# Hybrid pooling and attention block: a gate projection in another PSUM bank ahead of the last attention values, and the residual of the output projection loaded into its result tiles

## The chip, the cores and the metric

The kernel runs on one core of a Trainium2 chip. Its time is the device time of one execution in microseconds (us). The kernel before has a median of 2409.88 us over three runs (2409.58 to 2410.88). An execution that was recorded by the profiler gives the trace that all rows below come from. Engines are named as in the profile: PE is the matrix engine, PEld its weight load, DVE the vector engine, ACT the activation engine, POOL the general engine, SP the engine that issues most of the DMA transfers. SPq is the queue of SP: it issues in order, and a transfer that has to wait for a buffer holds up the transfers behind it.

## What is computed

One decoder block on x of 2048 positions by 1024 channels, all in float32. Cut to what matters here:

```python
h = rmsnorm(x, attn_norm)
z = h @ w_in                       # pool channels | q | k | v | gate_pool | gate_attn
gates = sigmoid(z[..., o4:] + b_gate)
g_pool, g_attn = gates[..., :D_MODEL], gates[..., D_MODEL:]
a = pool_mixer(u_pool, w_pool, pool_scale)      # causal means of 2, 4, 8, 16, minus the input
b = swa_sink_attention(q, k, v, sinks)          # window 128, 16 query heads, 2 key/value heads
x = x + (g_pool * a + g_attn * b) @ w_out
h = rmsnorm(x, ffn_norm)
up = causal_depthwise_conv(h @ w_up, conv_w, conv_b)
gate, val = up[..., :D_FF], up[..., D_FF:]
x = x + (silu(gate) * val) @ w_down
```

## The kernel before

**Chunks and precision.** The sequence goes through in two chunks of 1024 positions (`c` = 0 and 1). Activations lie with channels on the 128 partitions. To hold float32 precision every operand of a large product is split into a high part (a cast on ACT) and a low part (a subtraction on DVE), and each product is three matmuls, high by high, high by low, low by high (`mm3`, lines 257 to 263; `product`, lines 1166 to 1173). So every weight slab costs ACT and DVE work before PE can use it: `split` (lines 245 and 246), `halved` (358 and 359), the steps `second` and `fourth` of `Blocks` (374 to 379 and 386 to 388), `parted` (1043 and 1044) for activations.

**Attention.** `mixer` (from line 1656) runs 32 items, four groups of eight blocks (the last group is `group == 3`, its blocks are `n` = 0 to 7). For an item, `scores` makes the matmuls (873 to 879) and on DVE the mask, the maximum and two small operations (882 to 889; the last of these, line 889, is what `scores` returns as `chain`), then the exponentials on ACT (892) and the normalisation on DVE (898). `probabilities` of the item before transposes on PE (906), splits on ACT and DVE (908, 911) and makes a masked copy on POOL (914). `values` of the item two back multiplies with the values (934) into a bank of tag `"a"` and ACT copies it out (941). Between them stand fillers: projections such as `gated` (1007), which multiplies 24 matmuls into a bank of tag `"f"` (`project`, 689 to 697), and DVE and ACT then make tanh and `combine` from it (1015, 1016, 1023, 1024).

**Gates with fewer products.** The gates of the remaining channel tiles are computed two at a time by seven half-size products instead of eight (`Gates`, a subclass of `Up`: `one` to `seven`, lines 1191 to 1222). Each unit holds one bank of tag `"f"` from `one` to `seven`. Their right sides are differences of input blocks: `right_t1` (1133 to 1138) and `right_t2` to `right_t4`. In the first chunk two units start inside the last attention group, so both `"f"` banks are held when `gates` (from line 1411) begins. That function's head holds, in this order: the last filler (the plain gate `pg` of channel tile 4, first half; first chunk only), the last `probabilities`, the second half of `right_t1`, the last `values`, the loads of two input tiles, then the products `four`, `early`, `three` and so on. `values` of the item before the last stands ahead of all that, in `mixer` (1752).

**Order of the work.** The text's order gives priorities. A scheduler places each instruction of each engine in a fixed order when its inputs and its buffer are free by the scheduler's own reckoning, so an instruction whose buffer comes free late is placed behind others that stand after it in the text. `tc.issue_after(ins)` puts what is traced inside it behind `ins` on that instruction's engine.

**Output projection.** `out_proj` (1055 to 1116) runs two halves of 512 positions (`n`) by eight channel tiles (`m`). For each it loads a 128 by 512 residual `xr` of 256 KB from `xT` (1064, 1065, pool `fp`, tag `"F"`, four buffers), takes the split weights of `w_out` (three raw buffers of tag `"R"`, loaded three slabs ahead), makes 24 matmuls (1086), adds the residual on DVE (1090), scales into the result tile `xg` on ACT (1091; four tiles of 128 by 2 by 1024, pool `up_`, tag `"U"`, 19 buffers), squares it (647, 650), and stores it to `x2d` (1098). In the first chunk's first half it also makes the weights of two later units and stores them (1067 to 1076), which adds loads of `w_up` and stores to `kept`.

Of the kernel before, what the change touches and what calls it, by code (L numbers as in the profile page):

```python
# [16 lines left out]
F32 = mybir.dt.float32  # L17
# [9 lines left out]
P = 128  # L27
D = 1024
S = 2048
T = 1024  # L30
# [188 lines left out]
def block_kernel(ctx: ExitStack, tc: tile.TileContext, x, xT, pos, vec, qkn, w_poolT, w_pool, w_q, w_kv,  # L219
# [787 lines left out]
    def gated(c, ct, n, hs, ta, st):  # L1007
        if ("d", ct) not in st:
            st["pg"] = stream.get("pg", ct, later=later)
            st["t"] = fp.tile([P, T], F32, "F")  # L1010
            st["d", ct] = fp.tile([P, T], F32, "F")
            load(st["d", ct], dd[ct])
        pg, c_ = project(hs, st["pg"], n)
        d, t = st["d", ct][:, c_], st["t"][:, c_]
        V.tensor_mul(pg, pg, rB[:, c_])
        A.activation(t, pg, AF.Tanh, scale=0.5, bias=hbg[:, ct:ct + 1])
        later.append(lambda: combine(ct, n, t, ta, st))
# [37 lines left out]
    def out_proj(c, ms, mixes):  # L1055

        xg = [up_.tile([P, 2, T], F32, "U") for _ in range(4)]
        norms = []
        heads = [Kept(f) for f in PRE]
        for n in range(2):  # L1060
            acc = fp.tile([P, 512], F32, "F")
            c_ = slice(n * 512, (n + 1) * 512)
            for m in range(KT):
                xr = fp.tile([P, 512], F32, "F")
                load(xr, xT[m * P:(m + 1) * P, c * T + n * 512:c * T + (n + 1) * 512])
                w = stream.get("out", m)
                for f, at in PRE.items() if c == n == 0 else ():
                    if m == at:
                        raw = up_.tile([P, 2, 8, P], F32, "U")
                        load(raw[:, 0], w_up[f])  # L1070
                        load(raw[:, 1], w_up[FT + f])
                        made = Blocks([raw[:, 0], raw[:, 1]])
                    elif at < m < at + 3:
                        made.step(2)
                    elif m == at + 3:
                        made.store(f)
                if n == 0 and m == 3:
                    mixes[0] = mixed(0)
                if n == 0 and m > 3:
                    ms[7 - m].append(parted(mixes.pop(7 - m)[:, :, N1]))  # L1080
                if n == 1 and m >= 6:
                    heads[m - 6].fetch("A11", "A12")
                if n == 1 and m == 7:
                    stream.ahead().step(1)
                po = ps.tile([P, 512], F32, "f")
                mm3(po, [(w[:, 0, k, :], w[:, 1, k, :], ms[k // 2][n][:, 0, k % 2, :],
                          ms[k // 2][n][:, 1, k % 2, :])
                         for k in (6, 7, 4, 5, 2, 3, 0, 1)])
                x2 = mp.tile([P, 512], F32, "M")
                V.scalar_tensor_tensor(x2, po, 0.5, xr, op0=ALU.mult, op1=ALU.add)  # L1090
                A.activation(xg[m // 2][:, m % 2, c_], x2, AF.Identity,
                             scale=vc[:, V_FN + m:V_FN + m + 1])
                if m < 7 or n == 0:
                    square_in(acc, x2, m == 0)
                else:
                    sq = mp.tile([P, 512], F32, "M")
                    A.square(sq, x2)
                load(x2d[m][:, c_], x2)
                stream.part(stream.used + 2)
                if n == 1 and m == 1:  # L1100
                    norms[0]()
                if n == 1 and m == 3:
                    pb, b = norms[1](), {}
                if n == 1 and m >= 3 and m < 7:
                    right_first(xg, b, m - 3, pb)

            accs = [acc, sq] if n else [acc]

            def stats(n=n, accs=accs):
                rstd(accs, r2[:, 4 * n:4 * n + 4])  # L1110

            def whole(n=n):
                return spread(r2[:, 4 * n:4 * n + 4], None)

            norms += [stats, whole]
        return xg, b, norms[2:], heads
# [294 lines left out]
    def gates(c, units, b, xg, last_probabilities, last_values, last_filler):  # L1411
# [20 lines left out]
        else:  # L1432
            weights(1, 1)
            last_filler()
        last_probabilities()
        right_t1(xg, b, None, (1,))
        if c > 0:
            u2.two()
        last_values()
        run_later(9)  # L1440
        xg += [load_input(c, j) for j in (2, 3)]
        parts(0, "S3", "S2")
# [213 lines left out]
    def mixer(c, hs, kvw):  # L1656
# [49 lines left out]
        for i in range(len(items)):  # L1706
            group, n = divmod(i, NB)
            chain = scores(items[i])
            if i + 2 < len(items):
                load_queries(items[i + 2])  # L1710
            if i > 1:
                values(items[i - 2])
            run_later(0)
            fills = fillers(c, group)[n]
            last = chain
            for j, f in enumerate(fills):
                if i > 0 and j == (len(fills) > 1):
                    last = probabilities(items[i - 1], chain)
                if j == (len(fills) > 1):
                    run_later(2, last)  # L1720
                filler(*f, c, hs, ta, st)
            if group == 3:
                if c == 0:
                    if n == 0:
                        stream.fetch(stream.used + 2)
                    for f, steps in enumerate(({1: 1, 2: 2, 3: 1}, {5: 1, 6: 1})):
                        if n in steps:
                            units[f].w.step(steps[n])
                            units[f].w.store(units[f].f)
                    if n == 4:  # L1730
                        stream.fetch(stream.used + 1)
                elif n < 5:
                    if n == 2:
                        stream.fetch(stream.used + 2)
                    if n > 2:
                        units[n - 3].w = Kept(units[n - 3].f)
                        units[n - 3].w.fetch("A11", "A12")
                elif n == 5:
                    units[2].w = stream.get("gates", units[2].f)
                    units[2].w.step(1)  # L1740
                else:
                    units[n - 6].w.fetch("S1", "S4")
                if n in (4, 5):
                    xg.append(load_input(c, n - 4))
                if n == 5:
                    run_later(9)
                if n == 6:
                    scale_input(xg[0], 0)
                    right_t1(xg, b, None, (0,))
                if n == 7:  # L1750
                    scale_input(xg[1], 1)
        values(items[-2])
        run_later(9)
        return gates(c, units, b, xg, lambda: probabilities(items[-1]), lambda: values(items[-1]),
                     lambda: filler("pg", 4, 0, c, hs, ta, st))

    high, low = split_weights.last
    with tc.issue_after(low):
# [102 lines left out]
```

## Time and profile before

| | us |
|---|---|
| median of three runs | 2409.88 |
| the profiled execution's own time | 2411.6 |
| its span on the core | 2409.9 |
| PE busy in it | 2375.1 (99%) |
| DVE busy | 1885.8 (78%) |
| ACT busy | 1180.4 (49%) |
| POOL busy | 177.0 (7%) |

The span holds, in order: the first chunk's mixer to about 500 us, its output projection to 596, its up projection to about 1021 and the down projection to about 1233, and then the same for the second chunk, whose output projection lies between 1682 and 1771 us. In the rows of the profile, `[1.71 <-ACT U L245]` behind an instruction means that its engine was idle for 1.71 us before it and that an ACT instruction of line 245 ended that. "L" numbers are lines of the kernel. PEclk is the clock that PE was granted, 1.00 being full. An idle time under 0.15 us isn't shown as such.

### The profile page before, as it was taken

What the parts mean: (1) busy time and instruction counts of PE and PEld (TensorE: products, weight loads), DVE (VectorE), ACT (ScalarE), POOL (GpSimd) and SP (SyncE); (2) the same over time, 40 slices, a digit from 0 to 9 for tenths busy, and PEclk for the clock granted to TensorE, in tenths of its full rate; (3) what the DMA queues carried; (4) which work ended last, traced back from release to release, by engine and by line L of the source; (5) the groups of instructions that cost most, each with busy time, mean ns of one, the idle gap of its engine ahead of it and who ended that gap; (6) DMA issues with size and microseconds to landing.
All of it is one profiled execution on the core that took longest, in us unless ns stands there. A gap on an engine that the chain in (4) does not pass through costs nothing.

```text
span 2409.9 us, 30324 instructions
## 1 busy us (share of the span) xinstructions
PE 2375.1 (99%) x11120; PEld 1970.3 (82%) x11120; DVE 1885.8 (78%) x2916; ACT 1180.4 (49%) x2169; POOL 177.0 (7%) x122
## 2 busy tenths in 40 slices
PE   9999999999999999999999999999999999999999
PEld 8888887877888888788888888878888888888887
DVE  8687887876977777799945867787588777779994
ACT  7455455454555555543522544554546445554431
POOL 1123111000000000000002142200000000000000
PEclk9999999999999999999999999999999999999999
DMA  9767778588222333545244576665742222228421
GB/s 342 245 202 236 228 218 274 192 288 295 103 79 79 93 117 114 178 173 183 88 155 141 171 220 195 200 201 198 230 167 93 95 80 79 79 71 288 140 70 53
DMA packets 162597, 400.77 MB, mean 166 GB/s; under 512 B 14224, under 2 KB 50576, under 8 KB 152720
## 3 DMA queue, kind: packets, MB, share of 16 engines
q1 hardware_dynamic: 157664, 390.26, 47.8%
q0 software_dynamic: 4352, 8.39, 2.2%
q8 instruction: 87, 1.43, 0.2%
q14 instruction: 62, 0.51, 0.1%
q10 hardware_dynamic: 432, 0.19, 0.0%
HBM read 264.17 MB, written 134.61 MB: 165 GB/s over the span
## 4 chain that ended last, share of the span: by engine, by line
PE 53%; DMA 2%; DVE 2%; ACT 1%; issue 0%; POOL 0%; DVEq 0%; ACTq 0%; POOLq 0%; SPq 0%
PE f L262 11%; PE f L1170 11%; PE t L1170 6%; PE f L1637 4%; PE a L1637 4%; PE s L1637 4%; PE t L1637 4%; PE a L1170 3%; PE a L934 1%; PE a L262 1%; PE s L873 1%; DMA tad<-U 1%; PE t L906 0%; DMA U<-xT 0%; DMA F<-dd 0%; DMA U<-xd 0%
## 5 line engine op out<-in xcount | busy, mean ns | idle before, releaser
L262 PE MATMUL f<-U,U 128*128 128x512 f32 (+1 forms) x2880 | 674.5, 390 | 9.4 <-ACT U L245 5.3
L262 PEld LDWEIGHTS f<-U,U 128*128 128x128 f32 x2880 | 529.1, 188 | 120.5 <-ACT U L245 6.6
L1170 PE MATMUL f<-U,U 128*128 128x512 f32 x1872 | 446.9, 390 | 4.1 <-ACT Q L1188 3.8
L1170 PEld LDWEIGHTS f<-U,U 128*128 128x128 f32 x1872 | 350.4, 188 | 80.1 <-ACT Q L1188 6.0
L1236 DVE SCALAR_TENSOR_TENSOR M<-F,vc,M 128x1024 f32<-128x1024 f32 x176 | 225.1, 1281 | 140.8 <-ACT M L1233 140.5
L1170 PE MATMUL t<-U,U 128*128 128x512 f32 x1332 | 316.7, 391 | 0.6 <-ACT Q L1188 0.6
L1170 PEld LDWEIGHTS t<-U,U 128*128 128x128 f32 x1332 | 250.9, 189 | 53.3 <-ACT Q L1188 1.2
L358 ACT CAST U<-R 128x1024 fp32r<-128x1024 f32 x147 | 153.8, 1053 | 86.5 <-DVE R L387 42.3
L1170 PE MATMUL a<-U,U 128*128 128x512 f32 x756 | 183.9, 390 | 0.0
L359 DVE TENSOR_TENSOR U<-R,U 128x1024 fp32r<-128x1024 f32 x147 | 179.2, 1220 | 3.0 <-ACT U L358 3.0
L1170 PEld LDWEIGHTS a<-U,U 128*128 128x128 f32 x756 | 141.3, 188 | 29.4 <-ACT Q L1188 0.2
L1170 PE MATMUL f<-U,M 128*128 128x512 f32 x624 | 151.3, 390 | 2.1 <-DVE F L1214 2.0
L892 ACT ACTIVATE Q<-s,st,rq 128x128 f32<-128x128 f32 x256 | 113.7, 455 | 63.6 <-DVE st L889 63.2
L1170 PEld LDWEIGHTS f<-U,M 128*128 128x128 f32 x624 | 116.8, 188 | 27.7 <-DVE F L1214 3.6
L914 POOL TENSOR_SCALAR_AFFINE_SELECT M<-M 128x1024 fp32r<-128x1024 f32 x64 | 94.7, 1479 | 381.2 <-DVE st L894 245.0
L1222 ACT COPY F<-f 128x512 f32<-128x512 f32 x52 | 30.5, 586 | 182.7 <-PE f L1170 182.7
L1595 ACT CAST U<-U 128x1024 fp32r<-128x1024 f32 x76 | 79.0, 1051 | 83.4 <-PE s L1637 21.5
L1233 ACT ACTIVATE M<-F,vc 128x1024 f32<-128x1024 f32 x88 | 109.4, 1243 | 2.0 <-DVE F L1218 0.5
L1596 DVE TENSOR_TENSOR U<-U,U 128x1024 fp32r<-128x1024 f32 x76 | 91.9, 1218 | 2.8 <-ACT U L1595 2.6
L1595 ACT CAST F<-U 128x1024 fp32r<-128x1024 f32 x44 | 46.2, 1050 | 93.0 <-PE a L1637 63.5
L941 ACT COPY U<-a 128x512 f32<-128x512 f32 x64 | 37.6, 587 | 109.4 <-PE a L934 109.1
L1188 ACT COPY Q<-f 128x512 f32<-128x512 f32 x104 | 60.8, 585 | 50.8 <-PE f L1170 50.8
(281 smaller groups left out, 3728.5 us busy)
## 6 DMA issues: line engine op xcount, KB each, us to landing
R<-w_up SPq DMA_DIRECT2D x80, 512.0 KB, 3.7
actd<-M SPq DMA_DIRECT2D x44, 512.0 KB, 2.6
U<-w_down SPq DMA_DIRECT2D x88, 256.0 KB, 4.7
U<-actd SPq DMA_DIRECT2D x88, 256.0 KB, 5.0
qd<-U SPq DMA_DIRECT2D x64, 256.0 KB, 3.7
Q<-qd SPq DMA_DIRECT2D x64, 256.0 KB, 4.9
R<-w_out SPq DMA_DIRECT2D x32, 512.0 KB, 5.1
U<-kept_S SPq DMA_DIRECT2D x12, 1024.0 KB, 6.3
```

The source lines that it names most:

```text
L262: nc.tensor.matmul(out, a, b, start=(i == 0), stop=(i == n - 1))
L358: A.copy(t[:, 0], raw)
L359: V.tensor_sub(t[:, 1], raw, t[:, 0].bitcast(F32))
L892: A.activation(pr[:, h, :], sc[:, h, 0:P], AF.Exp, bias=nm[:, h:h + 1], scale=it["rq"][:, h:h + 1], accum_out=rs[:, h:h + 1])
L914: G.affine_select(own.rearrange("p a h q -> p (a h) q"), pa.bitcast(F32).rearrange("p a h q -> p (a h) q"), pattern=[[0, 8], [1, P]], base ...
L1170: nc.tensor.matmul(bank, a[:, x, k, :], b[k // 2][:, y, k % 2, :], start=(first and i == 0), stop=(i == 11), skip_group_check=True)
L1188: Up.last = A.copy(t, bank).ins
L1233: A.activation(y, u[:, 2:], AF.Identity, bias=cw[:, 3, m:m + 1], scale=cw[:, 2, m:m + 1])
L1236: V.scalar_tensor_tensor(y, u[:, j:j + T], cw[:, j, m:m + 1], y, op0=ALU.mult, op1=ALU.add)
L1595: A.copy(hi, src)
L1596: V.tensor_sub(lo, src, hi.bitcast(F32))
L1637: nc.tensor.matmul(into[m], u[:, 0, c_], v[:, 1], start=(first and j == 0), stop=(k == n - 1 and j == 2), skip_group_check=True)
```

## The change

Three edits, with the lines that they touch:

1. The last filler of the first chunk, the plain gate, projects into a bank of tag `"a"` in place of `"f"`. The `values` of the item before the last move from ahead of it to behind the last `probabilities`, in both chunks.
2. In the last attention group, the weight steps of the first two units are traced under `issue_after(chain)`; the second step of unit 1 moves from `n` = 6 to `n` = 7; the first half of `right_t1` moves from `n` = 6 to `n` = 7, behind `chain`. The move of `right_t1` holds for both chunks, the steps for the first.
3. In `out_proj`, both chunks, the 16 residual loads of 256 KB into `"F"` tiles go. In their place four loads of 1 MB fill the result tiles `xg` themselves, the first at the function's start and the others at `m` = 0, 2 and 4 of the first half; the addition reads the residual from there, and the scaling writes over it in place.

```diff
-        pg, c_ = project(hs, st["pg"], n)
+        pg, c_ = project(hs, st["pg"], n, st.pop("tag", "f"))
...
+        def residual(j):
+            load(xg[j], xT[2 * j * P:(2 * j + 2) * P, c * T:(c + 1) * T]
+                 .rearrange("(k p) t -> p k t", p=P))
+
+        residual(0)
         heads = [Kept(f) for f in PRE]
         for n in range(2):
...
             for m in range(KT):
-                xr = fp.tile([P, 512], F32, "F")
-                load(xr, xT[m * P:(m + 1) * P, c * T + n * 512:c * T + (n + 1) * 512])
+                if n == 0 and m % 2 == 0 and m < 6:
+                    residual(m // 2 + 1)
                 w = stream.get("out", m)
...
-                V.scalar_tensor_tensor(x2, po, 0.5, xr, op0=ALU.mult, op1=ALU.add)
+                V.scalar_tensor_tensor(x2, po, 0.5, xg[m // 2][:, m % 2, c_], op0=ALU.mult,
+                                       op1=ALU.add)
...
         last_probabilities()
+        last_values(-2)
+        run_later(9)
         right_t1(xg, b, None, (1,))
         if c > 0:
             u2.two()
-        last_values()
+        last_values(-1)
...
-                    for f, steps in enumerate(({1: 1, 2: 2, 3: 1}, {5: 1, 6: 1})):
+                    for f, steps in enumerate(({1: 1, 2: 2, 3: 1}, {5: 1, 7: 1})):
                         if n in steps:
-                            units[f].w.step(steps[n])
+                            with tc.issue_after(chain):
+                                units[f].w.step(steps[n])
...
                 if n == 6:
                     scale_input(xg[0], 0)
-                    right_t1(xg, b, None, (0,))
                 if n == 7:
+                    with tc.issue_after(chain):
+                        right_t1(xg, b, None, (0,))
                     scale_input(xg[1], 1)
-        values(items[-2])
-        run_later(9)
-        return gates(c, units, b, xg, lambda: probabilities(items[-1]), lambda: values(items[-1]),
-                     lambda: filler("pg", 4, 0, c, hs, ta, st))
+        return gates(c, units, b, xg, lambda: probabilities(items[-1]),
+                     lambda i: values(items[i]),
+                     lambda: filler("pg", 4, 0, c, hs, ta, dict(st, tag="a")))
```

## The prediction

> **What bounds the kernel.** I read the page first, then PE's waits in the stretch that the change touches, then the timelines of PE, DVE, POOL and SP around each wait, and last the granted clock.
>
> ```profile
> span 2409.9 us, 30324 instructions
> ...
> PE 2375.1 (99%) x11120; PEld 1970.3 (82%) x11120; DVE 1885.8 (78%) x2916; ACT 1180.4 (49%) x2169; POOL 177.0 (7%) x122
> ```
>
> PE is the bound: 2409.9 - 2375.1 leaves 34.8 us in the whole span in which it did nothing. So an edit can gain only by removing PE's idle time or time at a reduced clock, and loses by making either. The profiled execution took 2411.6 us, 1.7 more than its span and 1.7 more than the median of 2409.9; I make the sum as differences and apply it to the median. PE's waits between 340 and 600 us, from the last attention group of the first chunk to the end of its output projection (total, times, longest):
>
> ```profile
> PE f L262 <- ACT U L245: 5.3, 3, 1.9
> PE a L934 <- POOL M L914: 2.8, 1, 2.8
> PE f L1170 <- ACT Q L1188: 2.5, 2, 2.0
> PE f L262 <- DVE U L246: 2.1, 5, 0.9
> PE a L934 <- DVE M L911: 0.6, 1, 0.6
> PE f L1170 <- DVE U L1044: 0.3, 1, 0.3
> ```
>
> These are 13.6 of the 34.8 us, in a ninth of the span. Three places make them: the gates' head, the products behind it (L1188, L1044), and the output projection (L245, L246).
>
> **Part 1: the gates' head.** PE's timeline:
>
> ```profile
> 396.74 0.50 PE L934 MATMUL a<-M,U 128*128 128x512 f32 x1 [0.58 <-DVE M L911]
> 400.03 1.22 PE L934 MATMUL a<-M,U 128*128 128x512 f32 x2 [2.79 <-POOL M L914]
> ...
> 436.43 5.60 PE L262 MATMUL f<-U,U 128*128 128x512 f32 x24
> ```
>
> The two waits stand inside `values` of the item before the last. The 24 matmuls at 436.43 are the last filler, the plain gate. The text puts it ahead of those values, but both `"f"` banks belong to units 0 and 1 until a unit's `seven`, so it was placed 40 us late. While PE waits for POOL it has 5.6 us of work that only lacks a bank. Why the values were late:
>
> ```profile
> 392.32 0.69 DVE L882 COPY_PREDICATED s<-causal,s 128x512 f32<-128x512 uint8 x1
> ...
> 394.79 1.22 DVE L1137 TENSOR_TENSOR U<-U 128x1024 f32<-128x1024 f32 x1
> 395.93 0.15 DVE L889 TENSOR_TENSOR st<-st,vc 128x4 f32<-128x4 f32 x1
> 396.00 0.68 DVE L911 TENSOR_TENSOR M<-t,M 128x512 fp32r<-128x512 f32 x1
> ```
> ```profile
> 396.81 3.16 POOL L914 TENSOR_SCALAR_AFFINE_SELECT M<-M 128x1024 fp32r<-128x1024 f32 x1 [8.71 <-DVE st L894]
> ```
>
> From the mask (L882) to L889 DVE needed 3.6 us, because `right_t1` and weight steps were threaded in between; L911 came behind that, and POOL's select behind L911. The waits also cost clock. The next table cuts time into stretches of 3.41 us that end where the granted clock changes (PE busy, PEld, DVE, ACT, POOL, then PEclk):
>
> ```profile
> 395.78:399.20 3.42, 0.88 (x3) 0.19 (x1) 3.42 (x7) 3.27 (x12) 2.39 (x1) 1.00 0.57 170
> 399.20:402.60 3.40, 2.57 (x8) 1.97 (x9) 2.26 (x4) 1.16 (x3) 0.78 (x1) 0.50 1.01 395
> 402.60:406.03 3.43, 3.43 (x9) 2.66 (x9) 1.71 (x2) 2.32 (x3) 1.09 (x1) 0.50 0.53 203
> ...
> 419.68:423.09 3.41, 1.83 (x8) 1.52 (x9) 3.38 (x5) 3.41 (x4) 0.00 (x0) 1.00 0.01 1
> 545.97:549.38 3.41, 1.46 (x5) 0.93 (x6) 3.41 (x6) 3.41 (x7) 0.00 (x0) 1.00 1.06 435
> 549.38:552.80 3.42, 3.42 (x10) 2.65 (x9) 2.76 (x4) 1.29 (x3) 0.00 (x0) 0.50 0.99 401
> ```
>
> A stretch in which PE was busy 0.88 or 1.46 us of 3.4 is followed by half clock; one with 1.83 us isn't. At half clock PE was busy for 2.57 + 3.43 = 6.0 us here, of which half, 3.0 us, is lost. The head thus loses 0.58 + 2.79 + 3.0 = 6.4 us.
>
> With the gate in an `"a"` bank its matmuls start where PE began to wait, at 396.2, and last 5.6 us, past the end of the second wait at 400.0. DVE reaches L889 earlier as well, by up to the 1.22 us of L1137 and the weight steps behind it. So all 6.4 us go. What is late next: the gate no longer stands at 436, nor as a cushion, and PE comes earlier to the products behind the head, which waited 2.5 + 0.3 us there, with DVE all but full:
>
> ```profile
> 416.00:430.00 14.00, 11.21 (x47) 8.33 (x46) 13.28 (x14) 9.55 (x11) 0.00 (x0) 1.00 0.51 143
> ```
> ```profile
> 405.61 0.38 SPq L239 DMA_DIRECT2D U<-xT  x1
> ```
>
> PE loses 6.4 us less and does 5.6 us more there, so it is 0.8 us earlier at those products, with the gate behind it. The load at 405.61 that feeds their right sides waits for a `"U"` tile that the last values release, and so moves with PE; but DVE has to make the right sides in 94% of its time. The gate's own DVE work, three operations of the shape of L911 (0.68 us each), moves there too. I put 1.0 us of new wait on it. Bounds: nothing new and the old 2.8 us gone as well (a gain of 9.2), or DVE holds PE up for nearly all of it (a gain of 1). The value taken, 6.4 - 1.0 = **5.4 us gained**, is nearest to the row of the waits as they are, since their causes move with PE.
>
> The small moves. The `values` moved behind the transposes are four matmuls and one ACT copy; the bank that they need is that of unit 1's `two`, which DVE (L1200) reads while the gate runs. The last values need the gate's bank, which is free after the gate's tanh; PE has the moved values to do meanwhile. Unit 1's second step takes its 0.5 MB store with it; behind that on SPq stand a `w_ga` load for a later unit and an input load that waits on a buffer anyhow. `right_t1` issues no DMA; its tile is needed by `four`, which stands behind the gate and the values. All of these at nothing, hidden by the gate's 5.6 us; without that cover the delay of `right_t1`, two operations like L1137, would show as about 2.4 us.
>
> **Part 2: the output projection of the first chunk.** From SPq, the landing view of those two transfers (`xT`, then `w_out`), DVE, and PE:
>
> ```profile
> 521.96 0.94 SPq L239 DMA_DIRECT2D F<-xT  x1
> 522.94 0.58 SPq L239 DMA_DIRECT2D R<-w_out  x1
> ```
> ```profile
> DMA to landing us min/median/max: 8.3/8.3/8.3
> ```
> ```profile
> DMA to landing us min/median/max: 8.6/8.6/8.6
> ```
> ```profile
> 530.36 0.69 DVE L1090 SCALAR_TENSOR_TENSOR M<-f,F 128x512 f32<-128x512 f32 x1 [5.60 <-issue]
> ```
> ```profile
> 533.41 0.73 PE L262 MATMUL f<-U,U 128*128 128x512 f32 x2 [1.71 <-ACT U L245]
> 534.31 5.75 PE L262 MATMUL f<-U,U 128*128 128x512 f32 x24 [0.17 <-DVE U L246]
> 540.36 5.28 PE L262 MATMUL f<-U,U 128*128 128x512 f32 x22 [0.29 <-DVE U L246]
> 547.58 0.74 PE L262 MATMUL f<-U,U 128*128 128x512 f32 x2 [1.94 <-ACT U L245]
> 548.66 4.61 PE L262 MATMUL f<-U,U 128*128 128x512 f32 x12 [0.34 <-DVE U L246]
> ```
>
> The residual for `m` = 4 was issued at 521.96 and landed at 530.3; DVE's addition starts at 530.36 after 5.60 us of idle time that no engine ended. Behind it in DVE's and ACT's order stand the scaling and the splits of the next weights, so PE waits at 531.7. DVE then works off the backlog and PE waits again at 545.6, which is followed by 3.42 us at half clock, 1.7 us lost. Sum: 1.71 + 0.17 + 0.29 + 1.94 + 0.34 + 1.7 = 6.2 us. With `xg[2]` loaded from `m` = 2 on, its addition no longer waits, DVE has no backlog, and the second wait and the clock loss go. The first wait doesn't go wholly: `w_out` for `m` = 6 landed at 522.94 + 8.6 = 531.5, and its split can't start before; a first cast and subtraction, each taken as L911's 0.68, put it at 532.9, so 1.2 us stays. **Gain 5.0 us.** The bytes are the same, 4 MB per chunk, but 2 MB of the second half's loads now stand in the first, where there is little room:
>
> ```profile
> 511.00:534.00 23.00, 21.29 (x94) 17.12 (x92) 14.89 (x22) 11.72 (x19) 0.00 (x0) 1.00 1.00 373
> ```
>
> ```profile
> 491.33 1.25 SPq L239 DMA_DIRECT2D U<-w_up  x2
> ```
>
> The DMA engines are full from 511 to 534 at 373 GB/s; 1 MB more ahead of `w_out` costs 2.8 us there. The first load stands ahead of the `w_up` loads issued at 491.33, 20 us before that stretch, the second right behind them, and the third takes the place of the 256 KB loads of `m` = 1 to 3, so I expect the fourth at most to stand in the way. Bounds: a gain of 7 (all, with restarts), a loss of 9 (the last rival).
>
> **Part 3: the second chunk and the rest.** Its waits between 1540 and 1610 us:
>
> ```profile
> PE f L1170 <- DVE F L1214: 1.7, 1, 1.7
> PE a L934 <- POOL M L914: 1.0, 1, 1.0
> PE t L906 <- DVE Q L898: 0.7, 1, 0.7
> ```
>
> No plain gate stands here, so only the order changes. L898's wait should go with `right_t1` out of the chain; the others may shift. Gain 0.5, bounds 1.7 lost to 1.7 gained. Its output projection waits nowhere that the loads could relieve. The wait of the first chunk's other L245 (5.3 - 1.71 - 1.94 = 1.7 us) is behind weight steps that already came after their chain: nothing, within 2 us either way.
>
> **Sum.** 5.4 + 5.0 + 0.5 = 10.9 us off 2409.9: **2399.0 us**, by itself good for 2394.5 to 2403. What this kernel's measurement can tell from no change is about 0.2%, 4.8 us, so the border of faster is 2405.1.
>
> **Rivals.**
> *The loads stay in the way.* The fourth 1 MB load delays `w_out` of `m` = 6 by 2.8 us, and what the addition gains the split loses: part 2 gives nothing. For it: DMA share 1.00. Against it: the four loads can be issued before 511 if `"U"` tiles are free. 2409.9 - 5.9 = 2404.0. Chance 0.14.
> *The head gives little.* DVE (13.28 of 14 us) sets the pace behind the head, or the gate is still placed late. Part 1 gives 1: 2403.4. Chance 0.13. Both of these together: 2408.4, chance 0.06.
> *The clock isn't the waits' doing.* Then 3.0 + 1.7 us of half clock stay: 2399.0 + 4.7 = 2403.7. Against it: both stretches follow the two emptiest ones. Chance 0.04. The Trainium skill, TensorE: Matmul & The Clock Gate, section Part 1, lets the clock fall after at least one idle window of about 3.4 us; by that rule waits of 2.79 and 1.94 us would cost none. The trace has the length of the window but not the wholly idle one: PE was busy 0.88 and 1.46 us in them.
> *Slower.* The third or fourth load finds no free `"U"` tile, since mixes, split weights and stored weight blocks hold them, and SPq stands still until stores have landed. Behind it stands `w_out`. It decides from about 3 us of standstill: `w_out` then lands at 531.5 + 3 + 2.1 (0.75 MB more at 373 GB/s) = 536.6, the wait at 531.7 grows from 1.7 to about 6 and brings half clock for two stretches (3.4), and DVE's backlog keeps the second wait and adds 1.2. Part 2 loses 4.3 + 3.4 + 1.2 = 8.9, less parts 1 and 3: 2409.9 + 8.9 - 5.9 = 2412.9. Against it: the last unit's products release the eight tiles of T1 to T4 by the end of the mixer. Chance 0.07.
>
> **Numbers.** Forecast 0.56, rivals 0.14, 0.13, 0.06, 0.04, 0.07. The rivals at 2403.4 to 2404.0 lie near the border, a third of them beyond it: faster 0.78, within 0.2% 0.14, slower 0.08. The range goes from 2394 to 2408.
>
> **What would show it.** Right: the 24 matmuls of the gate stand in an `"a"` bank ahead of the values at about 396 to 402; no half clock between 395 and 410 or 540 and 560; L1090 at `m` = 4 not idle for 5 us; xT loads mostly ahead of 515. Wrong: a `w_out` load issued later than 525 or landing later than 534 for `m` = 6; a wait of over 4 us behind the head; a new half-clock stretch anywhere.

## The result and the profile after

The changed kernel has a median of 2415.66 us over 13 executions (2413.23 to 2418.73), the kernel before, run beside it, 2410.66 us (2408.69 to 2413.36). The ratio is 1.0022, its 95% interval 1.0013 to 1.0030: about 5 us slower, where 11 us faster was forecast and the range ended at 2408. The execution that was profiled took 2413.23 us, the lowest of the 13, with a span of 2411.5; its trace thus shows 1.6 us of the difference, and what the other executions have beyond that it can't show.

The page, first lines:

```profile
span 2411.5 us, 30292 instructions
...
PE 2374.3 (98%) x11120; PEld 1969.9 (82%) x11120; DVE 1886.6 (78%) x2916; ACT 1180.3 (49%) x2169; POOL 176.4 (7%) x122
```

PE is still the bound, with 37.2 us of idle time where it had 34.8. Lines behind the edits have other numbers: the residual's addition is L1096 now (it was L1090), the scaling L1098 (L1091), the product L1177 (L1170), `scale_input` L1415 (L1408). PE's timeline at the gates' head:

```profile
396.14 5.60 PE L262 MATMUL a<-U,U 128*128 128x512 f32 x24
...
406.38 0.74 PE L934 MATMUL a<-M,U 128*128 128x512 f32 x2 [0.21 <-POOL M L914]
...
424.23 0.80 PE L1177 MATMUL f<-U,U 128*128 128x512 f32 x1 [7.51 <-ACT U L1043]
```

The first two rows are as predicted: the plain gate stands at 396 in its new bank, and of the waits of 0.58 and 2.79 us in the values 0.21 is left. The third is new, a wait of 7.51 us behind the head, at a product of the units. It costs clock too. The stretches of 3.41 us (PE busy, PEld, DVE, ACT, POOL, then PEclk):

```profile
417.53:420.94 3.41, 0.00 (x0) 0.00 (x0) 1.04 (x1) 2.19 (x2) 0.00 (x0) 1.00 1.06 327
420.94:424.36 3.42, 0.13 (x1) 0.13 (x1) 3.42 (x4) 3.12 (x3) 0.00 (x0) 0.50 0.91 261
424.36:427.77 3.41, 2.69 (x6) 1.80 (x7) 3.41 (x4) 2.90 (x3) 0.00 (x0) 0.50 0.31 97
427.77:431.18 3.41, 3.41 (x10) 2.49 (x8) 3.41 (x4) 2.37 (x4) 0.00 (x0) 0.50 0.16 65
```

A stretch in which PE did nothing is followed by three at half clock, in the first of which PE was still almost idle. They hold 0.13 + 2.69 + 3.41 = 6.2 us of busy time, half of it lost: 3.1 us, as much as before at its own place (3.0). What PE waited for is seen by going back from it: ACT's and DVE's timelines, then SPq's.

```profile
417.62 2.19 ACT L1415 ACTIVATE U<-U,vc 128x1024 f32<-128x1024 f32 x2 [3.98 <-DMA U<-xT]
421.05 2.19 ACT L1415 ACTIVATE U<-U,vc 128x1024 f32<-128x1024 f32 x2 [1.25 <-DMA U<-xT]
```
```profile
407.33 0.74 DVE L1024 SCALAR_TENSOR_TENSOR U<-F,vc,U 128x512 f32<-128x512 f32 x1
419.90 1.23 DVE L1153 TENSOR_TENSOR M<-U,U 128x1024 f32<-128x1024 f32 x1 [11.83 <-ACT U L1415]
```
```profile
398.80 0.32 SPq L239 DMA_DIRECT2D kept_A<-M  x1
404.20 0.32 SPq L239 DMA_DIRECT2D kept_S<-U  x1
408.09 0.32 SPq L239 DMA_DIRECT2D xd<-U  x1
408.51 0.58 SPq L239 DMA_DIRECT2D tad<-U  x1
409.18 2.59 SPq L239 DMA_DIRECT2D U<-xT  x2
```

DVE, of which the prediction feared that it would be full, was idle for 11.83 us: it had nothing to make right sides from. The loads of the two input tiles were issued at 409.2 and 409.9 and took 8.4 and 11.2 us to land, until 417.6 and 421.1. In the kernel before the first was issued at 395.96, behind one store and one weight load, and the second at 405.61 (shown above), and each landed within 5.5 us:

```profile
390.69 0.33 SPq L239 DMA_DIRECT2D kept_A<-M  x1
391.08 0.42 SPq L239 DMA_DIRECT2D R<-w_ga  x1
395.96 0.38 SPq L239 DMA_DIRECT2D U<-xT  x1
397.92 0.33 SPq L239 DMA_DIRECT2D kept_S<-U  x1
```

The store at the head of both lists, `kept_A<-M`, is that of unit 1's second step. That step was moved behind the chain, its DVE work (L375) now starts at 398.08, and everything behind its store on SPq stands until then. Behind it follow two more stores that wait for DVE. `kept_S<-U`, of 1 MB, is that of unit 1's next step, `weights(1, 1)` at the head of `gates`; it works on what the second step leaves and was pushed back with it, from 397.92 to 404.20. `xd<-U` is the plain gate's, behind L1024 at 407.33, and comes earlier in the queue than before. SPq waited 12.4, 5.0 and 3.5 us for the DVE work of these three. In the kernel before the first input load stood ahead of `kept_S` and the second ahead of `tad`; now both stand behind all four stores.

The output projection of the first chunk. SPq, the landing view of `w_out` for `m` = 6, ACT and DVE:

```profile
525.43 1.39 SPq L239 DMA_DIRECT2D U<-xT  x1
526.87 1.35 SPq L239 DMA_DIRECT2D R<-w_out  x1
```
```profile
DMA to landing us min/median/max: 11.5/11.5/11.5
```
```profile
538.44 1.14 ACT L245 CAST U<-R 128x512 fp32r<-128x512 f32 x2 [4.77 <-DMA R<-w_out]
```
```profile
529.73 0.69 DVE L1096 SCALAR_TENSOR_TENSOR M<-f,U 128x512 f32<-128x512 f32 x1 [2.74 <-PE f L262]
```

The addition at `m` = 4 no longer waits for its residual (its 2.74 us are for PE), but the fourth 1 MB load stands in front of `w_out` for `m` = 6, which lands at 538.4 instead of 531.5, and now ACT waits 4.77 us for that. PE's waits from 490 to 620, the kernel before and the kernel after:

```profile
PE f L262 <- ACT U L245: 3.6, 2, 1.9
PE f L262 <- DVE U L246: 1.7, 4, 0.9
```
```profile
PE f L262 <- ACT U L245: 4.5, 2, 2.6
PE f L262 <- DVE M L1096: 0.8, 1, 0.8
PE f L262 <- DVE U L246: 0.8, 2, 0.4
```

5.3 us became 6.1, and one stretch at half clock (533.58 to 537.00) took the place of another: nothing won. In the second chunk the three waits of 3.4 us between 1540 and 1610 shrank to one:

```profile
PE a L1177 <- ACT Q L1195: 0.7, 1, 0.7
```

So the traces give PE 3.3 us more of waits from 340 to 470 us (11.6 where it had 8.3), 0.8 more in the first output projection, and 3.7 less from 1500 to 1800 (0.7 where it had 4.4). The rest of the 2.4 us of added idle time stands elsewhere, 1.2 of it ahead of 340 us.

### The profile page after: what moved, and what is told of

It is laid out like the page before. It is cut to its first block, busy times and chain, and to the rows that moved or that the text cites. A ratio compares the mean times of both kernels' runs of the same rounds, so it can differ in the third digit from the quotient of the medians.

```text
span 2411.5 us, 30292 instructions
## 1 busy us (share of the span) xinstructions
PE 2374.3 (98%) x11120; PEld 1969.9 (82%) x11120; DVE 1886.6 (78%) x2916; ACT 1180.3 (49%) x2169; POOL 176.4 (7%) x122
## 4 chain that ended last, share of the span: by engine, by line
PE 55%; DVE 1%; DMA 1%; ACT 0%; issue 0%; POOL 0%; SPq 0%; DVEq 0%; ACTq 0%; POOLq 0%
PE f L262 12%; PE f L1177 12%; PE t L1177 7%; PE f L1646 4%; PE a L1646 4%; PE s L1646 4%; PE t L1646 4%; PE a L1177 4%; PE a L934 1%; PE a L262 1%; PE s L873 1%; PE t L906 1%; DMA U<-made_pg 0%; DVE F L990 0%; ACT Q L892 0%; DMA U<-w_down 0%
## 5 line engine op out<-in xcount | busy, mean ns | idle before, releaser
L1177 PE MATMUL f<-U,U 128*128 128x512 f32 x1872 | 449.9, 391 | 9.6 <-ACT U L1043 7.5
L1177 PEld LDWEIGHTS f<-U,U 128*128 128x128 f32 x1872 | 352.6, 189 | 85.8 <-ACT U L1043 7.9
L1177 PE MATMUL t<-U,U 128*128 128x512 f32 x1332 | 315.0, 390 | 0.5 <-ACT Q L1195 0.4
L1177 PEld LDWEIGHTS t<-U,U 128*128 128x128 f32 x1332 | 249.5, 188 | 53.9 <-ACT Q L1195 1.2
L1177 PE MATMUL a<-U,U 128*128 128x512 f32 x756 | 184.3, 390 | 1.4 <-ACT Q L1195 1.4
L1177 PEld LDWEIGHTS a<-U,U 128*128 128x128 f32 x756 | 141.2, 188 | 31.6 <-ACT Q L1195 2.3
L1177 PE MATMUL f<-U,M 128*128 128x512 f32 x624 | 151.0, 389 | 0.3 <-DVE F L1221 0.3
L1177 PEld LDWEIGHTS f<-U,M 128*128 128x128 f32 x624 | 117.0, 188 | 25.0 <-DVE F L1221 0.8
L246 DVE TENSOR_TENSOR U<-R,U 128x512 fp32r<-128x512 f32 x122 | 82.9, 705 | 9.0 <-ACT U L245 8.7
```

Source lines behind the costliest of these rows:

```text
L246: low = V.tensor_sub(lo[:, t], src[:, t], hi[:, t].bitcast(F32))
L1177: nc.tensor.matmul(bank, a[:, x, k, :], b[k // 2][:, y, k % 2, :], start=(first and i == 0), stop=(i == 11), skip_group_check=True)
```

## The experiments

**The theory** for the head: the loss is SPq's order. The two input loads stand behind stores that wait for DVE work which the small moves delayed. **The rival**: DVE's pace behind the head, as the prediction had it. **For the output projection**: 2 MB of the second half's residual are brought into a stretch in which the DMA engines are full; its rival is the order of splits and scalings on ACT and DVE. All ran beside the kernel before, whose median was 2410.2 to 2410.9 in the four groups of runs; times are medians, ratios to the kernel before.

**The parts alone.** First the head's edits (1 and 2 of the change) without the residual's.

> Only the head's edits (gate's bank, order of the values, the moved steps); the residual is loaded as before. The theory: the two input loads stand on SPq behind unit 1's step store and behind the gate's own store, whose DVE work comes late now; so they are issued near 409 us again, PE waits about 7.5 us behind the head and gets half clock for three stretches. First chunk 3.7 us lost, second chunk 2.3 won: 2412 (2411 to 2414). The rival theory, DVE's pace behind the head, gives the same here. What the run tells is the share: if it is at 2410 or below, the head isn't where the change loses and the output projection is.

2412.04 us, ratio 1.0006 (0.9997 to 1.0015). The trace has the same queue (loads at 409.22) and the same wait (7.95 us at 424.63).

Then the residual's edit (3) alone.

> Only the residual's edit; the head as before. The theory: the addition at m = 4 no longer waits 5.6 us, but the fourth 1 MB load goes out ahead of w_out for m = 6 while the DMA engines are full, w_out lands 6 us later, and the output projection of the first chunk is worth nothing: 2411 (2409.5 to 2413). The rival: the order of splits and scalings on ACT and DVE makes the waits, not the landing; then the same time, but w_out lands by 533 and ACT still waits. If the run is over 2414, the residual's loads hold most of the whole change's loss, and the head little of it.

2412.19 us, 1.0011 (1.0002 to 1.0020). So neither part gains, and the losses of both, 1.5 and 1.7 us, come to 3.2, with the whole change's 5.0 within what the intervals of the two allow. In this run `w_out` for `m` = 6 landed 11.9 us after its issue, PE waited 2.88 us for its split, and its waits from 490 to 620 came to 7.1 us where the kernel before has 5.3.

**Which edit of the head.** The gate's bank alone, in the old order:

> Only the gate's bank; all written order as before, so the gate comes behind the values of the item before the last and can't fill the waits in them (0.6 and 2.8 us). The input loads keep their places on SPq ahead of the gate's store. By the queue theory nothing blocks them and the gate's 24 matmuls give DVE 5.6 us behind those values: the later waits go, the early ones and their half clock stay: 2408 (2406 to 2411). By the rival, DVE's pace, the products behind the head come 5.6 us of PE later anyhow and all of before's 2.8 us there goes: the same number; what tells is whether the trace shows the loads ahead of 407 and no wait over 2 us.

2410.74 us, 1.0001 (0.9992 to 1.0010), at the slow end of what was expected, and none of the 2.7 us hoped for. The waits of 0.60 and 2.79 us in the values stay, since the gate comes behind them, and the second load now waits for the gate's matmuls (11.3 us, until 411.75). The bank alone is worth nothing. The small moves alone:

> Only unit 1's second step and the transposed right side moved behind the chain; gate and values as before. By the queue theory the 0.5 MB store of that step now blocks the first input load (it waits for DVE until about 398), so both loads come later, the products behind the head wait 3 us or more beyond before's 2.8, and the waits in the values get shorter by what DVE has less to do: 2412 (2409 to 2416). By the rival, DVE's pace, taking DVE work out of the values' chain can only help: 2408 or less.

2415.07 us, 1.0019 (1.0011 to 1.0028), slower by 4.6 us: for the queue theory, and against the rival, by which less DVE work ahead could only help. The loads were issued at 399.23 and 406.61 here, 3.3 and 1.0 us later than in the kernel before. And the bank and the order of the values, without the moves and with the residual as before; against the change, steps and `right_t1` go back to their old places:

```diff
-                    for f, steps in enumerate(({1: 1, 2: 2, 3: 1}, {5: 1, 7: 1})):
+                    for f, steps in enumerate(({1: 1, 2: 2, 3: 1}, {5: 1, 6: 1})):
                         if n in steps:
-                            with tc.issue_after(chain):
-                                units[f].w.step(steps[n])
+                            units[f].w.step(steps[n])
...
                 if n == 6:
                     scale_input(xg[0], 0)
+                    right_t1(xg, b, None, (0,))
                 if n == 7:
-                    with tc.issue_after(chain):
-                        right_t1(xg, b, None, (0,))
```

> Gate in the other bank and ahead of the last values, but unit 1's second step and the transposed right side where they were before. By the queue theory the store of that step no longer stands in front of the input loads' time, the first is issued before 400 and the second before 407, both ahead of the gate's store; the wait behind the head is under 2.5 us and no half clock follows: 2406 (2404 to 2409). By the rival, DVE's pace: the gate's DVE work stands in front of the right sides as before, a wait of over 4 us stays, 2411 or more.

2401.82 us, 0.9964 (0.9950 to 0.9977): 8.7 us faster than before, 4 us more than expected, and 10.2 faster than with the moves. SPq:

```profile
392.43 0.33 SPq L239 DMA_DIRECT2D kept_A<-M  x1
...
397.69 0.38 SPq L239 DMA_DIRECT2D U<-xT  x1
...
403.14 0.38 SPq L239 DMA_DIRECT2D U<-xT  x1
407.06 0.33 SPq L239 DMA_DIRECT2D xd<-U  x1
```

The step's store is out at 392, the loads are in front of the gate's store, and the longest wait of PE from 395 to 435 is 0.37 us, the gate's DVE work notwithstanding. Which of the two moves does the harm: first the step alone added to that, with the steps of both units under `issue_after` as in the change.

> Gate in the other bank and ahead of the last values, and of the two small moves only unit 1's second step with its store; the transposed right side stays where it was. By the queue theory the step's store is what blocks: it stands in front of the first input load and waits for DVE until about 398, both loads come late, the long wait and the half clock are back: 2410 (2407 to 2413). By the rival, it is the transposed right side that comes late when it is moved, and this run stays at 2402 (2400 to 2404).

2410.28 us, 0.9995 (0.9987 to 1.0004), 8.5 us of the 10.2:

```profile
400.85 0.32 SPq L239 DMA_DIRECT2D kept_A<-M  x1
401.27 0.38 SPq L239 DMA_DIRECT2D U<-xT  x1
406.17 0.32 SPq L239 DMA_DIRECT2D kept_S<-U  x1
410.00 0.32 SPq L239 DMA_DIRECT2D xd<-U  x1
410.87 0.58 SPq L239 DMA_DIRECT2D tad<-U  x1
411.54 0.56 SPq L239 DMA_DIRECT2D U<-xT  x1
```
```profile
424.85 0.80 PE L1170 MATMUL f<-U,U 128*128 128x512 f32 x1 [4.35 <-ACT U L1043]
```

The step's store moved from 392.43 to 400.85, `kept_S` from 399.65 to 406.17, and the second load, now behind that store and two more, from 403.14 to 411.54. Then the transposed right side alone.

> Gate in the other bank and ahead of the last values, and of the two small moves only the transposed right side; unit 1's second step and its store stay where they were. By the queue theory the loads keep their early places (before 399 and before 406), no wait over 3 us stands behind the head, and the time is that without any move, 2402 (2400 to 2404). By the rival, the transposed right side that comes late costs the rest of the distance between the runs with no move and with both (10.2 us, of which the step alone made 8.5): 2404 to 2406.

2402.48 us, 0.9964 (0.9952 to 0.9977): within 0.7 us of the run without moves. The first load kept its place (396.29), the second missed it by 0.7 us (406.72, behind the gate's store at 406.35). In the second chunk, from 1500 to 1800, its waits are 1.7 us against 3.4 there, so the gain foreseen for that move is real, and in the first chunk about as much goes (PE waits 2.26 us for L1188 at 416.58). The harm comes with the moved step; whether by its stores on SPq or by its later DVE work, the next run tells.

**The loads first.** The head's edits with all moves, and one line put elsewhere in the first chunk:

```diff
+            xg += [load_input(c, j) for j in (2, 3)]
             weights(1, 1)
             last_filler()
...
-        xg += [load_input(c, j) for j in (2, 3)]
+        if c > 0:
+            xg += [load_input(c, j) for j in (2, 3)]
```

> The head's edits, and in the first chunk the two input loads written ahead of the last filler, so that on SPq they stand in front of unit 1's step store and of the gate's store. The residual as before. By the queue theory they are issued before 403, the wait of 7.5 us behind the head shrinks under 2 us, no half clock stands between 415 and 435, and the gain that was predicted for the head appears: 2404 (2402 to 2407). By the rival, DVE's pace, a wait over 4 us stays and the time is that of the head's edits alone, 2411 to 2413. A third way: no U tile is free so early, the load waits for one at the head of SPq and blocks the stores behind it: then 2412 or more, and the trace shows the load's issue waiting.

2396.82 us, 0.9947 (0.9934 to 0.9959): 13.4 us faster, and 7 us below what was expected. SPq, and PE's waits from 340 to 470:

```profile
389.62 5.19 SPq L239 DMA_DIRECT2D U<-xT  x2
399.34 0.34 SPq L239 DMA_DIRECT2D kept_A<-M  x1
405.31 0.34 SPq L239 DMA_DIRECT2D kept_S<-U  x1
```
```profile
PE f L262 <- ACT U L245: 1.8, 1, 1.8
PE a L934 <- POOL M L914: 0.4, 1, 0.4
```

The row of the loads holds both, at 389.6 and 394.4. The second did wait for a buffer at the head of SPq, 4.3 us, as the third way has it, but PE waited for nothing that stood behind it. The step's DVE work and its stores are as late as in the changed kernel (L375 at 398.62), only the loads no longer stand behind them: so it is the queue. DVE is as full from 420 to 435 as in the kernel before (14.94 us), and PE never waits for it there:

```profile
420.00:435.00 15.00, 15.00 (x67) 12.31 (x66) 14.66 (x18) 7.53 (x10) 0.00 (x0) 1.00 0.49 174
```

That is the end of the rival. Part of the 7 us beyond what was expected is luck: the output projection, which this run leaves as it was, waits 0.8 us less than in the kernel before and has none of its half clock (1.7 us). With the same code there, the other traces show none to two stretches at half clock. Another way to shorten the queue, the gate's combination with its store put behind `right_t2`:

> The head's edits, with the gate's combination and its store put behind the second transposed right side. The residual as before. By the queue theory the input loads then wait only for the steps' stores (issued at 398.8 and 404.2), go out near 404.5 instead of 409.2, and the wait behind the head shrinks from 7.5 to about 3 us with at most one half-clock stretch: 2408 (2406 to 2411). By the rival, DVE's pace, DVE has one operation of 0.7 us less ahead of the right sides: 0.7 us better than the head's edits alone.

2410.53 us, 1.0002 (0.9994 to 1.0011), against 2412.04 without it: hardly better. The time lies in the range that was expected, but of the shorter wait that was to bring it there is nothing. The gate's store is gone from the loads' front, but they are issued at 408.37 all the same, behind `tad<-U` at 407.68, the store of the attention output, and PE waits 7.25 us. The theory stands, the edit was a wrong reading of it: in a queue that stands, the next waiter takes over. Last, what the moves are worth when they can block nothing: the loads first, without moves.

> Gate in the other bank and ahead of the last values, input loads of the first chunk ahead of the last filler, no small move at all; the residual as before. It tells what the two moves are worth once they can't hold the loads up. If they bring the 2 us that the second chunk showed and what was hoped for the head: 2400 (2398 to 2402) here against 2396.8 with them. If they are worth nothing, 2397.

2401.18 us, 0.9960 (0.9946 to 0.9973), 4.4 us slower than with them. The profiled executions of the two are 2.0 us apart (2398.84 and 2396.82), and the second chunk's waits from 1500 to 1800 differ by as much, 3.7 us here and 1.7 with the moves; the rest lies in executions that have no trace.

**The output projection.** The residual's edit alone, with each load put behind the `w_out` load of its step:

> Only the residual's edit, with each load put behind the w_out load of its step. The head as before. By the theory w_out for m = 6 is issued ahead of the fourth residual load and lands by 532, ACT doesn't wait 4.8 us for it, and the output projection of the first chunk gains the 3 to 5 us that were predicted: 2407 (2405 to 2409). By the rival, the order on ACT and DVE, the waits stay and the time is that of the residual's edit alone, within 1 us.

2412.3 us, 1.0009 (1.0000 to 1.0019): no gain, and not the way that either side had it. `w_out` for `m` = 6 landed at 531.1 now, but then the residual behind it was late, and PE waited at its addition:

```profile
542.22 9.05 PE L262 MATMUL f<-U,U 128*128 128x512 f32 x26 [3.75 <-DVE M L1096]
```

So the order of the two isn't it; what comes last in this stretch waits. DMA share and GB/s from 490 to 545 us (the last two columns), the kernel before and the residual's edit as it is:

```profile
490.00:545.00 55.00, 52.81 (x229) 42.43 (x228) 42.13 (x59) 29.92 (x46) 0.00 (x0) 1.00 0.82 292
```
```profile
490.00:545.00 55.00, 50.11 (x217) 39.99 (x216) 39.50 (x56) 28.75 (x44) 0.00 (x0) 1.00 0.93 339
```

With this order it is 343 GB/s. 47 GB/s over 55 us are 2.6 MB more in this stretch. The next kernel is meant to take them out again; it loads the residual in halves, the second half of columns in the second pass over `m`:

```diff
+        def residual(i):
+            n, j = divmod(i, 4)
+            t = slice(c * T + n * 512, c * T + (n + 1) * 512)
+            load(xg[j][:, :, n * 512:(n + 1) * 512], xT[2 * j * P:(2 * j + 2) * P, t]
+                 .rearrange("(k p) t -> p k t", p=P))
...
+                if m % 2 == 0 and (n == 0 or m < 6):
+                    residual(4 * n + m // 2 + 1)
```

> Only the residual's edit, but each 1 MB load cut into its two halves of columns, the second half loaded in the second pass over m. The head as before. The theory: the edit loses because it brings 2 MB of the second pass forward into the stretch from 490 to 545 us, where the DMA engines are full (292 GB/s before, 339 with the edit); with the bytes where they were, w_out for m = 6 lands by 533, the addition at m = 4 doesn't wait 5.6 us, and of before's 9.0 us lost there 4 go: 2406.5 (2404 to 2409). The rival, the order of splits and scalings on ACT and DVE: within 1 us of the residual's edit as it is, 2412.

2407.9 us, 0.9988 (0.9979 to 0.9997): faster by 3 us, and 4.3 us better than with whole tiles. `w_out` for `m` = 6, issued at 523.26, landed in 6.9 us where it took 11.9, and PE's waits from 490 to 620 fell to

```profile
PE f L262 <- ACT U L245: 1.9, 1, 1.9
PE f L262 <- DVE U L246: 1.4, 3, 0.6
```

That was the gain sought, at three fifths of its size. 2.0 us of it are these waits; one stretch at half clock stays, from 546.88 to 550.30. The theory is supported, not shown: from 490 to 545 us this run still moved 318 GB/s, 26 more than the kernel before, and with the bytes it also halves the single load ahead of `w_out`. Which of the two counts no run parts. Then the parts put together: the whole change with its loads first,

> The whole change with one line moved: the two input loads of the first chunk ahead of the last filler. By the queue theory the place of these loads on SPq is all that kept the change from its head's gain: the head gives what it gave without the residual, and the residual costs its 1 to 2 us: 2398.5 (2396 to 2401). If something else in the change holds the time up, 2404 or more.

2402.38 us, 0.9966 (0.9954 to 0.9979), and the same with the residual in halves,

> The head's edits with the input loads written ahead of the last filler, and the residual loaded in halves. If both causes are what the theory says, the gains add up: 2396.8 less 3.7, 2393 (2390 to 2397). If the halves bring nothing: 2397 to 2399.

2397.14 us, 0.9943 (0.9931 to 0.9956). The one line makes the change 13.3 us faster; the residual in whole tiles costs 5.6 us there (4.8 with each run against its own kernel before; expected were 1 to 2), with `w_out` for `m` = 6 landing 13.5 us after its issue:

```profile
530.73 13.24 PE L262 MATMUL f<-U,U 128*128 128x512 f32 x48 [6.33 <-ACT U L245]
```

In halves it costs nothing (landing 6.3 us), but it doesn't gain its 3 us a second time either, against what was expected: 2397.14 against 2396.82. With the loads first, the old residual loads have `w_out` down in 7.2 us as well. The version to keep is the one with the loads first and the old residual, or with halves; the two can't be told apart.

## Why the prediction was wrong

**The small moves** are the step that failed. It said that unit 1's second step "takes its 0.5 MB store with it; behind that on SPq stand a `w_ga` load for a later unit and an input load that waits on a buffer anyhow", and put "All of these at nothing, hidden by the gate's 5.6 us". The store was named and the queue read, and the cost still set at nothing. Three things were wrong in that. The input load behind the store, issued at 395.96, did wait on a buffer (SPq waited 4.4 us for a product of PE, L1170), but it had it at 395.9, and the moved store went at 398.80. The step takes a second store with it that wasn't counted, the 1 MB of `kept_S`, which went at 404.20. And hiding on PE was no cover, since what waited was SP. With the change the loads left at 409.2 and 409.9 where they had left at 395.96 and 405.61. The run with only the step moved costs 8.5 us, the one with only the transposed right side 0.7. Who stands behind the store was asked; it had to be answered for every load, with the time at which it was needed.

**The gates' head.** What the prediction said of the gate itself was right: its place, the two waits and the half clock at 399 to 406 gone. "The load at 405.61 that feeds their right sides waits for a `"U"` tile that the last values release, and so moves with PE" is right for the kernel before, where SPq waited 6.9 us for the last values (L934), but the load didn't move with PE: in the changed kernel it went later while PE came earlier, since it waited for the stores ahead and for no tile. With the loads out of the queue's way, the waits from 340 to 470 fall from 8.3 to 2.2 us and the 3.0 us of half clock go, 9.1 us, close to the upper bound of 9.2, where 5.4 was forecast. 1.7 us of this are lost again in that trace to a new stretch at half clock from 352.73 to 356.14, ahead of the head. DVE at 94% was feared for 1 us of wait, and in that run nothing of it came.

**The output projection.** The addition's wait went, as said. The rival "The loads stay in the way" was the right mechanism, with its sign and its place (the fourth load, `w_out` of `m` = 6); its price, 2.8 us of delay, was too small. The landing came 6.8 us later: 3.9 by the later issue and 2.9 by the longer way (11.5 against 8.6 us). It was weighed at 0.14 because "the four loads can be issued before 511"; three were (495.47, 495.95 and 509.34), the fourth at 525.43, since the text holds it at `m` = 4, where on SPq it stands behind the store of the result before (`x2d`, 525.01), which waits for its addition on DVE (L1096 at 524.29). The bytes of the second pass that the edit brings forward were counted ("2 MB of the second half's loads now stand in the first"), but not charged in the sum.

**"Slower"** was forecast through SPq standing still for a tile, in part 2. SPq did stand, but for DVE, and in part 1. **The clock** behaved as in the table of the prediction where PE was nearly idle: half clock followed each stretch with up to 1.49 us of busy PE in all sixteen traces, and the rival that half clock isn't the waits' doing falls with the run with the loads first, which has neither waits nor half clock at the head. In the output projection of the changed kernel the stretch ahead of the half clock was this:

```profile
530.17:533.58 3.41, 1.25 (x4) 0.77 (x5) 2.11 (x4) 3.12 (x5) 0.00 (x0) 1.00 0.99 395
```

PE was busy for 1.25 us of it. The Trainium skill, TensorE: Matmul & The Clock Gate, section Part 1, has the clock fall after at least one idle window of about 3.4 us; the length agrees, but no wholly idle window was needed here. Above 1.49 us busy time alone doesn't decide: 1.64 us from 349.31 in the run with the loads first were followed by half clock, 1.63 us from 349.26 in the changed kernel weren't, and 2.50 us from 563.28 in the run with the head's edits alone were.

**The second chunk** was forecast at 0.5 us and gave 2.7 by its waits from 1540 to 1610 us, 3.7 from 1500 to 1800. The runs with and without the transposed right side moved put 1.7 to 2.0 us of this down to that move.

**What stays open.** The profiled execution of the changed kernel shows 1.6 of the 5.0 us. Why other executions of the same kernel are up to 5.5 us longer no trace here shows. But each has its mean granted clock on record: 0.997 in the profiled one, 0.996 in eight of the others and 0.995 in four. With PE busy all the while, 0.001 of 2411 us is 2.4 us (an estimate), so more time at half clock can make most of the rest; which waits bring it stays open. Whether it is the bytes or the size of the loads that delays `w_out` is open too. And the scheduler's order on ACT, which in the changed kernel puts the split of `w_out` for `m` = 5 behind the scaling of `m` = 4 (a wait of 2.56 us at 532.26), was changed in no run by itself.

## What to carry to other kernels

A step that is moved takes its stores with it, and a store that waits holds up every load behind it on an in-order queue: list for the new place all that stands behind it, with the time at which each was issued and is needed, before calling the move free. Loads that a later stage needs belong in front of stores that nobody waits for, where their buffers come free in time. And a load made larger to save waits elsewhere has its own price where the DMA engines are full: the bytes that it brings forward, and the delay of the load behind it.

## What the runs showed of the hardware that was not expected

The issue of a transfer isn't of one length. The 1 MB load at 405.61 in the kernel before kept SPq busy for 0.38 us; the pair at 409.18 in the changed kernel took 0.58 and 1.92 us, and `w_out` at 526.87 took 1.35 us where the same load at 522.94 in the kernel before took 0.58. A full DMA stretch alone doesn't do it, for at 522.94 the share was 1.00 as well; the issues of 1.92 and 1.35 us stood right behind a 1 MB load that hadn't landed, that of 0.58 at 522.94 behind one of 256 KB. What decides it no run here tests, but it delays whatever stands behind on the queue.

And the clock comes back later than it falls. A stretch with 2.57 us (399.20, the kernel before) or 2.69 us of busy PE (424.36, the changed kernel) at half clock was followed by another at half clock, and so was one with 2.73 us (402.32, the gate's bank alone). Those with 3.07 us (354.28, the whole change with its loads first) or more were followed by full clock, while at full clock 1.83 us had been enough to keep it.

The same wait doesn't cost the same each time. PE waits 1.7 to 1.8 us for L245 at about 352 us in all sixteen traces. In six of them, the run with the loads first among them, a stretch at half clock follows, which costs up to 1.7 us; in ten, the kernel before and the changed kernel among them, none does.
